# Weight splits ordered behind the attention steps, and output projections on spare wide PSUM tiles, in a streaming encoder on one core

## The chip, the cores and the metric

The program runs on one core of a Trainium2 chip. A core has a matmul engine, TensorE (PE, with its weight loads listed as PEld), and the engines VectorE (DVE), ScalarE (ACT), GpSimd (POOL) and SyncE (SP), each with an instruction stream of its own that it works through in order. They wait for each other by semaphores. PE writes its results to PSUM, which DVE and ACT read. The metric is the device time of one execution in microseconds. Before the change three executions took 1470.21, 1471.60 and 1471.62 us, a median of 1471.6.

## The reference

Two layers over 512 frames of one new stream and 16 frames of each of 8 running streams (640 columns in all, width 1024). The first layer is a convolution module, the second is chunked attention with 16 heads of 64; a SwiGLU feed-forward follows each. Everything is in float32. The attention layer, which is what the change touches, is this:

```
k, v = jnp.split(rms_norm(h, norm_kv) @ w_kv, 2, axis=-1)
q = (rms_norm(h, norm_attn[j]) @ w_q[j]).reshape(B, T, N_HEADS, HEAD_DIM)
s = einsum(q, k) * scale + bias        # own chunk of 64 frames and the 8 before
p = softmax(s)                         # chunks before the stream's start masked
o = einsum(p, v)
h = h + o @ w_o[j]
h = swiglu_ffn(h, norm_ffn[l], w_ffn_in[l], w_ffn_out[l])
```

The running streams attend to 512 cached rows of k and v each beside their own 16.

## The kernel before

Products in float32 accuracy are made of three matmuls on split operands: each weight w becomes `whi` (ACT, rounded) and `wlo` = w - `whi` (DVE), each activation `xh` and `xl`, and PE adds up whi·xh, wlo·xh and whi·xl. The residual stream `h` lies in SBUF as 8 tiles of 128 rows by 640 columns.

The attention layer goes through the 16 heads in 8 pairs, p = 0 to 7. The projections of pair 0 (k0, q0) and of the first group of values (v0) are made ahead. The others are made beside the attention: `SETS` lists 13 sets of weights, k (keys and queries of one pair), v (values of two pairs) and o (the output projection of two pairs, added to `h`). `stream()` is a generator that goes through them; each step of it issues one **piece** of PE's work on the present set and one or two pieces of the next set's split. The split is in `pieces()`: one DMA brings 1 MB of weights into `raw`, then 16 pieces of 128 columns (k) or 8 of 256 (v and o) go through `whi` on ACT (L1272 where the weight has no gain, L1276 where it has) and `wlo` on DVE (L1273, L1277). A k set has 12 pieces of PE's work, v 15, o 16 (one for each of 8 row tiles and two halves of 320 columns); a piece of o is six matmuls of 320 columns (L1259), a piece of k at most nine matmuls of 256 or 384.

`BO` is the order of one pair, and `FILL` says how many pieces go into each of the 8 pairs. In `BO`, f4 is "up to four pieces", f* "all that are left", and the rest are attention steps:

- A: `heads()`, the scores of both heads on two wide PSUM tiles and two narrow ones (L1396), from `KH`, `KL`, `QH`, `QL`, the split k and q of the pair (L1376, L1377). Then on DVE the bias and the row maximum (L1198) and `nb` (L1188), on ACT the exps (L1191), on DVE the scaling of `S` by `rs` (L1412).
- s0, s1: the scores of the running streams on a wide tile each (`Sn`, `Ss`, L1459, L1462).
- b00 to b12: transposes of `S` (L1425), copied to `PT` by ACT (L1429) or DVE (L1431).
- t0, t1 and n0, n1: transposes of `Sn` and `Ss` (L1475, L1481), copied to `PTs` by ACT (L1486) and to `PM` and `PN` by DVE (L1483).
- P, c, d: the products with the values (L1441, L1497), the last transpose (L1506), and the split of the result into `ohi` and `olo` (L187, L189).

PE's order is fixed by hand: each step is issued behind the last matmul of the step before (`pe()`, `step_end`). On the other engines a scheduler places the instructions by priority; the copies marked `high_priority` come first, the split pieces and the softmax come as the data allows. PSUM has two wide tiles (1024 columns, `w2t()`), two narrow tiles `mm` of 512 columns for the pieces (`mmt()`), and two `am` for transposes and the like. Between the step s1 and the next A no attention step uses the wide tiles. A piece of o takes an `mm` tile, and DVE adds it to `h` (L1344). At its first call, `stream()` loads the first set and splits all of it (`load(0)` and eight steps): the 16 pieces of k1. The last o set (o3) is made by `halves()` behind pair 7, on `mm` and `am` tiles; its `wlo` is one instruction of 2048 columns (L180).

With the sums of `FILL` (20, 42, 63, 87, 111, 137, 165, 177) and the sizes of the sets (k1 to 12, v1 to 27, k2 to 39, k3 to 51, o0 to 67, k4 to 79, v2 to 94, k5 to 106, o1 to 122, k6 to 134, v3 to 149, k7 to 161, o2 to 177), o0 lies with 12 pieces in pair 2 and 4 in pair 3, o1 with 5 in pair 4 and 11 in pair 5, o2 with 4 in pair 6 and 12 in pair 7.

Of the kernel before, what the change touches and what calls it, by code (L numbers as in the profile page):

```python
# [8 lines left out]
F32 = mybir.dt.float32  # L9
# [3 lines left out]
ALU = mybir.AluOpType  # L13
# [69 lines left out]
def tile_trunk(ctx, tc, xT, vecs, hist, w_pw1, w_pw2, w_in0, w_out0, w_os0, w_in1, w_out1, w_os1,  # L83
# [1101 lines left out]
    def softmax_rows(S, mx, sm, tiles):  # L1185
        k = len(tiles)
        nb = ap.tile([P, 4], F32, tag="nb", name=nm("nb"), bufs=3)
        nc.vector.tensor_scalar(out=nb[:, :k], in0=mx[:, :k], scalar1=-0.125, scalar2=None,  # L1188
                                op0=ALU.mult)
        for i, (o, n) in enumerate(tiles):  # L1190
            nc.scalar.activation(out=S[:, o:o + n], in_=S[:, o:o + n], func=AF.Exp, scale=0.125,  # L1191
                                 bias=nb[:, i:i + 1], accum_out=sm[:, i:i + 1])
# [9 lines left out]
    fill, step_end = None, [None]  # L1202

    def proj_kq(p):
        wh, wl = wsplit(w_kq[p], 16, P, gains=GKQ)
# [58 lines left out]
    def pieces(w, src, gains, n):  # L1264
        raw, hi, lo = (wp.tile([P, 2048], F32 if t == "raw" else F32R, tag=t, name=nm(t))
                       for t in ("raw", "whi", "wlo"))
        w += [hi, lo]
        nc.sync.dma_start(raw, src if len(src.shape) == 2 else src.rearrange("p m c -> p (m c)"))
        gains = gains or [(a, a + 256, None) for a in range(0, 2048, 256)]
        for i, (a, b, gain) in enumerate(gains):  # L1270
            if gain is None:
                nc.scalar.activation(out=hi[:, a:b], in_=raw[:, a:b], func=AF.Copy)  # L1272
                nc.vector.tensor_tensor(out=lo[:, a:b], in0=raw[:, a:b],  # L1273
                                        in1=hi[:, a:b].bitcast(F32), op=ALU.subtract)
            else:
                nc.scalar.activation(out=hi[:, a:b], in_=raw[:, a:b], func=AF.Copy, scale=gain)  # L1276
                nc.vector.scalar_tensor_tensor(out=lo[:, a:b], in0=raw[:, a:b], scalar=gain,  # L1277
                                               in1=hi[:, a:b].bitcast(F32), op0=ALU.mult,
                                               op1=ALU.subtract)
            if i % n == n - 1:  # L1280
                yield
        while True:
            yield

    def set_kq(p, w):
        wh, wl = w
        kt = op_.tile([P, NT], F32, tag="kt", name=nm("kt"), bufs=2)
        qt = op_.tile([P, NT], F32, tag="qt", name=nm("qt"), bufs=QB)
        kts[p], qts[p] = kt, qt
        for g, (g0, n) in enumerate(GR):  # L1290
            for t, dst in enumerate((kt, qt)):
                pt = mmt()
                for a, b in zip(PARTS, PARTS[1:]):
                    mm3_part(pt[:, :n], [(wh[:, (2 * k + t) * P:(2 * k + t + 1) * P],
                                          wl[:, (2 * k + t) * P:(2 * k + t + 1) * P])
                                         for k in range(KT)], xk(xs[g], range(KT)), a, b)
                    if b == KT:
                        with tc.high_priority(offset=HP):
                            nc.vector.tensor_tensor(out=dst[:, g0:g0 + n], in0=pt[:, :n],
                                                    in1=xs[g][2], op=ALU.mult)  # L1300
                            if g == 0 and t:
                                for hh in range(2):
                                    r = slice(hh * DH, hh * DH + DH)
                                    nc.gpsimd.tensor_copy(
                                        qbd[p % 2][r, :, hh, :],
                                        qt[r, 0:P].rearrange("p (b q) -> p b q", q=SB))
                        if g and t:
                            nc.sync.dma_start(k_out[p], kt)
                            split[p] = heads_split(p)
                    yield  # L1310

    def set_v(r, w):
        wh, wl = w
        VT = ap.tile([P, 5, 256], F32, tag="vt", name=nm("vt"), bufs=2)
        vts[r] = VT
        for tt in range(5):
            g = 0 if tt < 2 else 1
            c0 = tt * P - GR[g][0]
            pt = mmt()
            for a, b in zip(PARTS, PARTS[1:]):  # L1320
                mm3_part(pt[:, :256], [(xs[g][0][:, k, c0:c0 + P], xs[g][1][:, k, c0:c0 + P])
                                       for k in range(KT)],
                         [(wh[:, k * 256:(k + 1) * 256], wl[:, k * 256:(k + 1) * 256])
                          for k in range(KT)], a, b)
                if b == KT:
                    with tc.high_priority(offset=HP):
                        nc.scalar.activation(out=VT[:, tt, :], in_=pt[:, :256], func=AF.Copy,
                                             scale=xs[g][3][:, c0 // P:c0 // P + 1])
                    if tt == 4:
                        nc.sync.dma_start(v_out[:, :, r * 256:r * 256 + 256], VT)  # L1330
                yield

    def set_o(r, w):
        wh, wl = w
        for g0 in (0, NH):
            for m in range(KT):
                pt = mmt()
                mm3_part(pt[:, :NH], [(wh[:, (k * 8 + m) * P:(k * 8 + m + 1) * P],
                                       wl[:, (k * 8 + m) * P:(k * 8 + m + 1) * P])
                                      for k in range(2)],  # L1340
                         [(oT[2 * r + k][0][:, g0:g0 + NH], oT[2 * r + k][1][:, g0:g0 + NH])
                          for k in range(2)], 0, 2)
                with tc.high_priority(offset=HP):
                    nc.vector.tensor_tensor(out=h[:, m, g0:g0 + NH], in0=pt[:, :NH],  # L1344
                                            in1=h[:, m, g0:g0 + NH], op=ALU.add)
                yield
# [25 lines left out]
    def heads_split(p):  # L1372
        ts = [ap.tile([P, 512], F32R, tag=t, name=nm(t)) for t in ("KH", "KL", "QH", "QL")]
        with tc.high_priority(offset=HP):
            for src, hi, lo in ((kts[p], *ts[:2]), (qts[p], *ts[2:])):
                nc.scalar.activation(out=hi, in_=src[:, P:], func=AF.Copy)  # L1376
                nc.vector.tensor_tensor(out=lo, in0=src[:, P:], in1=hi.bitcast(F32),  # L1377
                                        op=ALU.subtract)
        return ts

    def heads(ts):
# [18 lines left out]
    def head_a(p, hh, pss):  # L1400
        S = sp.tile([P, 1280], F32, tag="S", name=nm("S"))
        mx = ap.tile([P, 4], F32, tag="mx", name=nm("mx"), bufs=3)
        sm = ap.tile([P, 4], F32, tag="sm", name=nm("sm"), bufs=3)
        for ii, i in enumerate(ORD):
            n = (i + 1) * P
            o = SOFF[i]
            addmax(S[:, o:o + n], pss[ii], BP[:, hh, 512 - n:512], mx[:, ii:ii + 1])
        rs = softmax_rows(S, mx, sm, [(SOFF[i], (i + 1) * P) for i in ORD])
        for ii, i in enumerate(ORD):
            n = (i + 1) * P  # L1410
            o = SOFF[i]
            nc.vector.tensor_scalar(out=S[:, o:o + n], in0=S[:, o:o + n],  # L1412
                                    scalar1=rs[:, ii:ii + 1], scalar2=None, op0=ALU.mult)
        return S

    def head_b(S, PT, j):
# [9 lines left out]
                        tr[:, o:o + P], S[:, SOFF[i] + k * P:SOFF[i] + (k + 1) * P], ident).ins  # L1426
                tot += P
        if j == 0:
            nc.scalar.activation(out=PT[:, base:base + tot], in_=tr[:, :tot], func=AF.Copy)  # L1429
        else:  # L1430
            nc.vector.tensor_copy(PT[:, base:base + tot], tr[:, :tot])  # L1431

    def pair_c(p, PTs):
        VT = vts[p // 2]
# [103 lines left out]
    for p in range(NP):  # L1538
# [8 lines left out]
        for op in BO.split():  # L1547
# [7 lines left out]
            i = int(op[1]) if len(op) > 1 else None  # L1555
            with pe(), tc.high_priority(offset=HP):
                if op[0] == "A":
                    pss = heads(split[p])
                    ha = {hh: head_a(p, hh, pss[hh]) for hh in range(2)}
                    pt = {hh: sp.tile([P, 1280], F32, tag="PT", name=nm("PT")) for hh in range(2)}  # L1560
# [11 lines left out]
                    ps[i]()  # L1572
                else:
                    pair_c(p, (pt[0], pt[1]))
            if op == "s1" and p + 1 < NP:
                bias_load(p + 1)

    next(fill, None)
    adds = []
# [228 lines left out]
```

## Time and profile before

| what | us |
|---|---|
| median of three runs | 1471.6 |
| profiled execution, own time | 1470.02 |
| its span | 1468.2 |
| PE busy in it | 1429.5 |
| attention stage, 691 to 1012 | 321.0, of which PE is busy 303.5 |

The other stages are the convolution layer and its feed-forward ahead of 633 us, the projections of pair 0 to 699, and the second feed-forward from about 1030 to the end. The granted clock over the span is 0.997 of the full one.

In the rows that follow, a row of a timeline gives start, duration, engine, line, operation, output<-inputs, shape and count, and in brackets the idle time of the engine just before it with what ended it. A row of instruction groups ends in busy time, mean duration in ns, and the idle time before the group with what released it. A row of waits gives engine, tile and line that waited, what for, and the total in us, the number of times and the longest. PE's durations overlap: the next matmul is issued before the last one ends.

### The profile page before, as it was taken

To read this page: it belongs to the slowest core of one execution; us is meant where nothing else is said; L and a number is where in the kernel's file an instruction comes from. 1 tells how busy PE (TensorE), PEld (TensorE's weight loads), DVE (VectorE), ACT (ScalarE), POOL (GpSimd) and SP (SyncE) were. 2 spreads that over 40 slices of the span, in tenths; PEclk is the share of its full clock that TensorE was granted. 3 is DMA by queue.
4 is the path that set the end of the run, shared out by engine and by line. 5 is a ranking of instruction groups with operands and counts; after the bars stand their busy time and mean duration, and the time that the engine had idled before them with its cause. 6 is when DMAs were issued, how large, how long until landed. Compare 5 with 4: busy or idle time off the path is not lost.

```text
span 1468.2 us, 28278 instructions
## 1 busy us (share of the span) xinstructions
PE 1429.5 (97%) x11086; PEld 1368.3 (93%) x11086; DVE 1119.1 (76%) x2509; ACT 748.2 (51%) x1633; POOL 281.5 (19%) x335
## 2 busy tenths in 40 slices
PE   9999999999999999999999999998999999999998
PEld 8998799999999999999888888887999999999998
DVE  6789767988788888666557657556899888788755
ACT  5666554554554554454544544433554455465453
POOL 5799130011110111012111111101001111111101
PEclk9999999999999999999999999999999999999999
DMA  7267434044545444415565464542124544544522
GB/s 242 85 172 185 120 87 144 19 134 144 133 107 149 130 110 121 137 58 200 172 201 163 157 208 156 187 143 62 68 77 133 137 118 125 144 120 108 157 63 72
DMA packets 66933, 192.58 MB, mean 131 GB/s; under 512 B 12144, under 2 KB 30320, under 8 KB 58480
## 3 DMA queue, kind: packets, MB, share of 16 engines
q1 hardware_dynamic: 52432, 160.58, 33.7%
q0 software_dynamic: 13504, 29.37, 10.1%
q8 instruction: 87, 1.43, 0.4%
q10 hardware_dynamic: 864, 0.83, 0.2%
q14 instruction: 46, 0.38, 0.1%
HBM read 179.14 MB, written 11.61 MB: 130 GB/s over the span
## 4 chain that ended last, share of the span: by engine, by line
PE 81%; DVE 10%; ACT 3%; DMA 3%; issue 1%; POOL 1%; DVEq 0%; ACTq 0%; POOLq 0%
PE mm L439 44%; PE mm L1259 9%; PE mm L199 6%; PE mm L200 6%; PE mm L201 6%; PE mm L885 2%; DMA raw<-in_w_os 2%; DVE wlo L372 1%; DMA raw<-in_w_in 1%; PE am L1441 1%; PE am L1497 1%; ACT whi L1276 1%; PE am L1425 1%; PE mm L146 1%; ACT S L1191 1%
## 5 line engine op out<-in xcount | busy, mean ns | idle before, releaser
L439 PE MATMUL mm<-XH,whi 128*128 128x320 f32 x896 | 276.0, 310 | 2.6 <-ACT t L451 2.6
L439 PE MATMUL mm<-XH,wlo 128*128 128x320 f32 x896 | 276.4, 309 | 0.0
L439 PE MATMUL mm<-XL,whi 128*128 128x320 f32 x896 | 274.7, 309 | 0.0
L371 ACT ACTIVATE whi<-raw 128x512 fp32r<-128x512 f32 (+2 forms) x280 | 168.4, 613 | 140.8 <-PE mm L439 107.4
L372 DVE TENSOR_TENSOR wlo<-raw,whi 128x512 fp32r<-128x512 f32 (+2 forms) x280 | 184.5, 667 | 19.0 <-ACT whi L371 17.9
L439 PE MATMUL mm<-hid,whi 128*128 128x320 f32 x732 | 172.0, 311 | 3.1 <-DVE hid L372 2.2
L439 PEld LDWEIGHTS mm<-XH,whi 128*128 128x128 f32 x896 | 167.8, 188 | 4.2 <-ACT t L451 4.2
L439 PEld LDWEIGHTS mm<-XH,wlo 128*128 128x128 f32 x896 | 168.3, 188 | 0.0
L439 PEld LDWEIGHTS mm<-XL,whi 128*128 128x128 f32 x896 | 167.8, 188 | 0.0
L439 PEld LDWEIGHTS mm<-hid,whi 128*128 128x128 f32 x732 | 125.0, 188 | 5.9 <-DVE hid L372 3.3
L199 PE MATMUL mm<-xh,whi 128*128 128x320 f32 (+2 forms) x416 | 129.2, 312 | 0.8 <-DVE h L702 0.4
L200 PE MATMUL mm<-xh,wlo 128*128 128x320 f32 (+2 forms) x416 | 128.1, 310 | 0.0
L201 PE MATMUL mm<-xl,whi 128*128 128x320 f32 (+2 forms) x416 | 126.0, 310 | 0.0
L439 PE MATMUL mm<-hid,wlo 128*128 128x320 f32 x366 | 113.1, 309 | 0.0
L439 PE MATMUL mm<-XH,shi 128*128 128x320 f32 x344 | 106.0, 309 | 0.7 <-DVE h L1528 0.7
L439 PE MATMUL mm<-XH,slo 128*128 128x320 f32 x344 | 106.1, 308 | 0.0
L439 PE MATMUL mm<-XL,shi 128*128 128x320 f32 x344 | 105.6, 308 | 0.0
L841 POOL TENSOR_TENSOR ca<-ca,cvt 128x512 f32<-128x512 f32 x60 | 91.9, 1531 | 16.3 <-ACT cvt L838 9.8
L417 POOL DMA_DIRECT2D s<-in_w_in x38 | 22.0, 580 | 377.1 <-DVE wlo L372 153.3
L371 ACT ACTIVATE shi<-raw 128x512 fp32r<-128x512 f32 (+1 forms) x114 | 66.7, 588 | 44.2 <-PE mm L439 39.3
L580 DVE TENSOR_TENSOR h<-h,mm 128x320 f32<-128x320 f32 x168 | 79.8, 480 | 4.3 <-PE mm L439 4.0
L451 ACT ACTIVATE t<-mm 128x320 f32<-128x320 f32 x114 | 49.5, 434 | 62.3 <-PE mm L439 61.9
(324 smaller groups left out, 3697.1 us busy)
## 6 DMA issues: line engine op xcount, KB each, us to landing
raw<-in_w_in SPq DMA_DIRECT2D x38, 1024.0 KB
s<-in_w_in POOLq DMA_DIRECT2D x76, 256.0 KB, 4.2
raw<-in_w_os SPq DMA_DIRECT2D x24, 768.0 KB
cache<-in_ck SPq DMA_DIRECT2D x32, 512.0 KB
cache<-in_cv SPq DMA_DIRECT2D x32, 512.0 KB
raw<-in_w_pw SPq DMA_DIRECT2D x11, 1024.0 KB
s<-in_w_os POOLq DMA_DIRECT2D x48, 192.0 KB, 3.6
raw<-in_w_kq SPq DMA_DIRECT2D x8, 1024.0 KB
```

Source lines behind the costliest of these rows:

```text
L199: nc.tensor.matmul(ps, wh, xh, start=(first and i == 0), stop=False)
L200: nc.tensor.matmul(ps, wl, xh, start=False, stop=False)
L201: end = nc.tensor.matmul(ps, wh, xl, start=False, stop=(stop and i == last))
L371: put_end[1] = nc.scalar.activation(out=hi, in_=src, func=AF.Copy).ins
L372: put_end[0] = nc.vector.tensor_tensor(out=lo, in0=src, in1=hi.bitcast(F32), op=sub).ins
L417: nc.gpsimd.dma_start(s1, src[:, 2 * n:3 * n])
L439: last = nc.tensor.matmul(pt, wt, v, start=(first and k == i == 0), stop=(k == n - 1 and i == 2), skip_group_check=True)
L451: keeps.append(nc.scalar.activation(out=t, in_=pt, func=AF.Copy).ins)
L580: nc.vector.tensor_tensor(out=hv, in0=hv, in1=pt, op=sub if row else add)
L841: nc.gpsimd.tensor_tensor(out=acc, in0=acc, in1=pr, op=ALU.add)
L885: conv_end[0] = nc.tensor.matmul(pt[32 * q:32 * q + 32, 0:n], w4[0:r, 4 * tg + q, :], mv, start=(tg == 0), stop=(tg == 7)).ins
L1259: step_end[0] = nc.tensor.matmul(ps, w, x, start=i == j == 0, stop=i == len(wts) - 1 and j == 2).ins
```

## The change

`note()` keeps, for each engine, the last instruction of the attention steps: the exps, the copies of `kt`, `qt` and `vt`, `KH`, `KL`, `QH`, `QL`, the scaling of `S` and the copies to `PT`. Each split piece is issued behind those kept ones (`behind`: an order on its own engine and against the others in the scheduler, with no semaphore of its own). Not kept are the copies to `PTs`, `PM` and `PN`, the bias and maximum, `ohi` and `olo`, and the adds to `h`. `set_o()` takes halves of a wide tile instead of an `mm` tile from the step s1 until the next A. `FILL` moves the sets between the pairs: its sums are now 20, 39, 67, 94, 122, 142, 165, 177, so that o0 lies wholly at the end of pair 2, o1 at the end of pair 4, and o2 as before.

```
-FILL = 20, 22, 21, 24, 24, 26, 28, 12
+FILL = 20, 19, 28, 27, 28, 20, 23, 12
...
-            nc.scalar.activation(out=S[:, o:o + n], in_=S[:, o:o + n], func=AF.Exp, scale=0.125,
-                                 bias=nb[:, i:i + 1], accum_out=sm[:, i:i + 1])
+            note(nc.scalar.activation(out=S[:, o:o + n], in_=S[:, o:o + n], func=AF.Exp,
+                                      scale=0.125, bias=nb[:, i:i + 1],
+                                      accum_out=sm[:, i:i + 1]))
...
+    fill, step_end, spare_w2 = None, [None], [None, []]
+    ahead = {}
+
+    def note(ins):
+        ahead[ins.ins.engine] = ins.ins
+        return ins
...
+            with behind(*ahead.values()):
+                if gain is None:
+                    nc.scalar.activation(out=hi[:, a:b], in_=raw[:, a:b], func=AF.Copy)
+                    nc.vector.tensor_tensor(out=lo[:, a:b], in0=raw[:, a:b],
+                                            in1=hi[:, a:b].bitcast(F32), op=ALU.subtract)
...
-                pt = mmt()
+                if spare_w2[0]:
+                    if not spare_w2[1]:
+                        t = w2t()
+                        spare_w2[1] += [t[:, 0:512], t[:, 512:1024]]
+                    pt = spare_w2[1].pop(0)
+                else:
+                    pt = mmt()
...
                 if op[0] == "A":
+                    spare_w2[:] = False, []
                     pss = heads(split[p])
...
+            if op == "s1":
+                spare_w2[0] = True
+                if p + 1 < NP:
+                    bias_load(p + 1)
```

The lines behind the edits move: L1259 becomes L1265, L1276 and L1277 become L1283 and L1284, L1272 becomes L1279, L1344 becomes L1357, L1376 and L1377 become L1389 and L1390, L1396 becomes L1409, L1425 becomes L1438, L1431 becomes L1444, L1486 becomes L1499.

ACT's order around pair 0's heads, before. `KH_7837` and `QH_7839` are the split k and q of pair 0, `whi_7952` is k1, `whi_8000` is v1, `S_7911` and `S_7930` are the scores of the two heads:

```order
L1376 ACTIVATE KH_7837<-kt_7576 128x512
L1276 ACTIVATE whi_7952<-raw_7951,vec 128x128 x12
L1376 ACTIVATE QH_7839<-qt_7577 128x512
L1276 ACTIVATE whi_7952<-raw_7951,vec 128x128 x4
L1238 ACTIVATE vt_7652<-mm_7758,rt_7465 128x256
L1238 ACTIVATE vt_7652<-mm_7784,rt_7465 128x256
L1276 ACTIVATE whi_8000<-raw_7999,vec 128x256 x2
L1238 ACTIVATE vt_7652<-mm_7810,rt_7465 128x256
L1191 ACT_TABLE_LOAD
L1191 ACTIVATE S_7911,sm_7913<-S_7911,nb_7918 128x512
```

The same engine and tiles in the changed kernel, from the second head's exps on (ahead of these rows stand `KH_7837`, `QH_7839`, two copies to `vt`, the table load and the five exps that come first):

```order
L1191 ACTIVATE S_7930,sm_7932<-S_7930,nb_7937 128x384
L1191 ACTIVATE S_7930,sm_7932<-S_7930,nb_7937 128x128
L1191 ACTIVATE S_7930,sm_7932<-S_7930,nb_7937 128x256
L1244 ACTIVATE vt_7652<-mm_7810,rt_7465 128x256
L1283 ACTIVATE whi_7952<-raw_7951,vec 128x128 x16
L1283 ACTIVATE whi_8000<-raw_7999,vec 128x256 x4
L1191 ACTIVATE Sn,sm_8047<-Sn,nb_8049 128x576
```

All 16 pieces of k1 have moved from ahead of the exps to behind them. DVE's `wlo` pieces have moved likewise, from ahead of the bias and maximum to behind the scaling of both heads. On PE the heads of pair 0 stand 16 matmuls earlier in the product of v0's fourth tile; the k1 matmuls stand where they stood, right behind v0's last.

ACT's order at the end of pair 2, before: `QH_9165` is the split q of the next pair, `whi_9184` the next set of weights, `PTs_9248` and `PTs_9267` the copies for the running streams:

```order
L1376 ACTIVATE KH_9163<-kt_8875 128x512
L1429 ACTIVATE PT_9003<-am_9134 128x512
L1276 ACTIVATE whi_9184<-raw_9183,vec 128x128 x12
L1376 ACTIVATE QH_9165<-qt_8876 128x512
L1276 ACTIVATE whi_9184<-raw_9183,vec 128x128 x4
L1429 ACTIVATE PT_9004<-am_9191 128x512
L1486 ACTIVATE PTs_9248<-am_9243 128x512
L1486 ACTIVATE PTs_9267<-am_9262 128x512
```

The same place in the changed kernel, with `whi_9200` as the next set and `PTs_9212` and `PTs_9230` as the copies:

```order
L1389 ACTIVATE KH_9179<-kt_8967 128x512
L1442 ACTIVATE PT_8966<-am_9150 128x512
L1389 ACTIVATE QH_9181<-qt_8968 128x512
L1283 ACTIVATE whi_9200<-raw_9199,vec 128x128 x13
L1499 ACTIVATE PTs_9212<-am_9207 128x512
L1283 ACTIVATE whi_9200<-raw_9199,vec 128x128 x3
L1499 ACTIVATE PTs_9230<-am_9225 128x512
```

`QH` and the second `PT` are now ahead of the pieces, and both `PTs` have pieces ahead of them, the first all thirteen.

PE's order in the pieces of o0, before. `mm_9505` and `mm_9513` are the PSUM tiles of two pieces that follow each other, `ohi` and `olo` the attention's split results:

```order
L1259 MATMUL mm_9505<-olo_7866,whi_8888 128x320
L1259 MATMUL mm_9505<-ohi_8407,whi_8888 128x320
L1259 MATMUL mm_9505<-ohi_8407,wlo_8889 128x320
L1259 MATMUL mm_9505<-olo_8408,whi_8888 128x320
L1259 MATMUL mm_9513<-ohi_7865,whi_8888 128x320 [waits DVE_49]
L1259 MATMUL mm_9513<-ohi_7865,wlo_8889 128x320
```

The pieces of o0 in the changed kernel, late in pair 2. `w_1016_9405` is a wide tile, and both halves of it carry its name:

```order
L1265 MATMUL w_1016_9405<-olo_7866,whi_8980 128x320
L1265 MATMUL w_1016_9405<-ohi_8407,whi_8980 128x320
L1265 MATMUL w_1016_9405<-ohi_8407,wlo_8981 128x320
L1265 MATMUL w_1016_9405<-olo_8408,whi_8980 128x320
L1265 MATMUL w_1016_9405<-ohi_7865,whi_8980 128x320 [waits DVE_49]
L1265 MATMUL w_1016_9405<-ohi_7865,wlo_8981 128x320
```

Before, the wait is for the add that reads the tile of the piece before the last one, since two `mm` tiles take turns. In the changed kernel the first matmul of the second half waits for the add that reads the first half of the same tile, because a wide tile is tracked as one. The next wide tile starts without a wait of its own.

More of the change, by code (lines that the diff above doesn't have):

```diff
@@ L1270, in pieces @@
         for i, (a, b, gain) in enumerate(gains):
[L1271 to L1279, printed above, removed]
+            with behind(*ahead.values()):
[4 more added lines that the diff above has]
+                else:
+                    nc.scalar.activation(out=hi[:, a:b], in_=raw[:, a:b], func=AF.Copy, scale=gain)
+                    nc.vector.scalar_tensor_tensor(out=lo[:, a:b], in0=raw[:, a:b], scalar=gain,
+                                                   in1=hi[:, a:b].bitcast(F32), op0=ALU.mult,
+                                                   op1=ALU.subtract)
             if i % n == n - 1:
@@ L1375, in heads_split @@
             for src, hi, lo in ((kts[p], *ts[:2]), (qts[p], *ts[2:])):
-                nc.scalar.activation(out=hi, in_=src[:, P:], func=AF.Copy)
-                nc.vector.tensor_tensor(out=lo, in0=src[:, P:], in1=hi.bitcast(F32),
-                                        op=ALU.subtract)
+                note(nc.scalar.activation(out=hi, in_=src[:, P:], func=AF.Copy))
+                note(nc.vector.tensor_tensor(out=lo, in0=src[:, P:], in1=hi.bitcast(F32),
+                                             op=ALU.subtract))
         return ts
@@ L1411, in head_a @@
             o = SOFF[i]
[L1412 to L1413 removed]
+            note(nc.vector.tensor_scalar(out=S[:, o:o + n], in0=S[:, o:o + n],
+                                         scalar1=rs[:, ii:ii + 1], scalar2=None, op0=ALU.mult))
         return S
```

16 lines of the change are left out of this document (7 added, 9 removed).

## The prediction

> **What bounds the kernel now.** I read the page's busy shares and its chain first, then the busy time of the attention stage by pair of heads, then what TensorE (PE) waited for there. The page:
>
> ```profile
> PE 1429.5 (97%) x11086; PEld 1368.3 (93%) x11086; DVE 1119.1 (76%) x2509; ACT 748.2 (51%) x1633; POOL 281.5 (19%) x335
> ...
> PE 81%; DVE 10%; ACT 3%; DMA 3%; issue 1%; POOL 1%; DVEq 0%; ACTq 0%; POOLq 0%
> ```
>
> PE is busy for 97% of the span. The diff touches only code between the first attention pair and the norm behind the last, so I took that stretch cut at the first head matmul of each pair 0 to 7 (columns: length, busy time of PE, PEld, DVE, ACT, POOL, granted clock, DMA share, GB/s):
>
> ```profile
> 693.00:735.00 42.00, 39.92 (x371) 35.00 (x370) 23.88 (x80) 21.85 (x59) 6.07 (x11) 0.96 0.53 172
> 735.00:773.00 38.00, 37.63 (x367) 33.34 (x365) 22.88 (x80) 19.26 (x60) 5.42 (x11) 1.00 0.63 211
> 773.00:811.00 38.00, 36.15 (x332) 31.05 (x334) 26.48 (x86) 16.17 (x49) 5.39 (x11) 1.00 0.52 164
> 811.00:853.00 42.00, 39.23 (x372) 34.66 (x370) 25.71 (x85) 19.61 (x58) 6.53 (x11) 1.00 0.54 186
> 853.00:892.00 39.00, 38.80 (x366) 34.13 (x364) 22.62 (x75) 18.38 (x56) 5.75 (x11) 1.00 0.52 172
> 892.00:937.00 45.00, 41.06 (x372) 36.10 (x370) 29.57 (x96) 18.93 (x55) 5.85 (x11) 1.00 0.47 156
> 937.00:981.00 44.00, 43.19 (x402) 38.64 (x402) 23.75 (x71) 18.51 (x49) 5.50 (x11) 1.00 0.54 173
> 981.00:1013.00 32.00, 26.46 (x266) 21.58 (x267) 19.39 (x64) 12.41 (x33) 3.04 (x4) 1.00 0.33 83
> ```
>
> Length less PE's busy time gives PE's idle time: 2.1, 0.4, 1.9, 2.8, 0.2, 3.9, 0.8 and 5.5 us, 17.6 us in all. That is everything the change can win by covering waits. What ended those waits (total, times, longest):
>
> ```profile
> PE mm L1259 <- DVE h L1344: 4.9, 4, 1.7
> PE am L1481 <- ACT PTs L1486: 2.8, 4, 1.9
> PE w L1396 <- DVE QL L1377: 2.2, 4, 1.2
> PE mm L1259 <- DVE nb L1188: 1.6, 2, 1.4
> PE w L1396 <- ACT QH L1376: 1.6, 2, 1.4
> ```
>
> They are what the change aims at: a projection piece that waits for the residual add h of an earlier piece, a transpose that waits for PTs, heads that wait for QH and QL, each with weight splits or softmax work ahead of it on ACT or DVE. PE issues in a fixed order, so each such wait delays all the rest. A wait costs a little more than its idle time:
>
> ```profile
> 814.48 0.31 PE L1259 MATMUL mm<-olo,whi 128*128 128x320 f32 x1
> 816.41 0.41 PE L1259 MATMUL mm<-ohi,whi 128*128 128x320 f32 x1 [1.62 <-DVE h L1344]
> ```
>
> These starts lie 1.93 us apart where the rows above them lie 0.147 apart (six matmuls, one piece, in 0.88 us): 1.78 us lost for 1.62 idle. So I add 0.16 us for each wait.
>
> **The change, part by part.** The same matmuls run; no work is added. Three things move.
>
> *First, the pieces of k1.* Before, they stood ahead of pair 0's softmax on ACT (twelve, QH, then four) and on DVE. The rows, of ACT, DVE and PE:
>
> ```profile
> 687.95 3.63 ACT L1276 ACTIVATE whi<-raw,vec 128x128 fp32r<-128x128 f32 x12 [2.79 <-PE mm L201]
> 691.49 0.62 ACT L1376 ACTIVATE QH<-qt 128x512 fp32r<-128x512 f32 x1
> ...
> 698.81 0.29 DVE L1188 TENSOR_SCALAR nb<-mx 128x4 f32<-128x4 f32 x2
> 699.56 0.45 ACT L1238 ACTIVATE vt<-mm,rt 128x256 f32<-128x256 f32 x1
> 700.03 1.28 ACT L1191 ACT_TABLE_LOAD   x1
> 701.33 0.72 ACT L1191 ACTIVATE S<-S,nb 128x512 f32<-128x512 f32 x1
> 705.62 0.18 ACT L1191 ACTIVATION_READ_ACCUMULATOR S<-S,nb 128x1 f32 x1
> 703.86 1.28 DVE L1412 TENSOR_SCALAR S<-S,rs 128x512 f32<-128x512 f32 x4
> 698.54 0.28 PE L201 MATMUL mm<-wlo,xh 128*128 128x256 f32 x1
> ```
>
> In the changed order all 16 stand behind both heads' exps on ACT and behind both heads' scalings on DVE, while PE's k1 matmuls still follow its last v0 matmul. PE is free there at 698.54 + 0.12 = 698.66. QH no longer waits behind twelve pieces, and the order shows the heads 16 matmuls earlier, 1.8 us; nb is ready near 697.3 then. Table load 1.28, the eight exps 705.80 - 701.33 = 4.47, a value copy 0.45: the first whi lands near 703.9. DVE scales the second head after its last exp (0.2 + 1.28) and makes the first wlo (0.35) by about 705.0; the second matmul needs it. PE waits about 5.2 us for whi and 0.9 more for wlo: **+6.1 us**. Ends: 4.9 (the wlo wait hidden) and 7.9 (heads where they stood). Everything on PE stands behind it. Afterwards pieces come every 0.30 us and PE takes one in 0.36, so it is not held again; the PTs wait of this pair, 1.9 us in 2.1 idle, goes (**-2.4**, two waits).
>
> A long gap also has a price in clock. PE's gap for PTs in pair 0 was followed by this (columns of the stretches as above):
>
> ```profile
> 723.13 0.33 PE L1481 MATMUL am<-ident,Sn 128*128 128x128 f32 x1 [1.93 <-ACT PTs L1486]
> ```
>
> ```profile
> 722.00:724.00 2.00, 0.71 (x4) 0.53 (x5) 1.52 (x7) 1.92 (x6) 0.00 (x0) 1.00 0.00 0
> 724.00:726.00 2.00, 2.00 (x11) 1.62 (x11) 0.27 (x1) 0.00 (x0) 0.00 (x0) 0.53 0.89 213
> 726.00:728.00 2.00, 2.00 (x8) 0.61 (x6) 0.00 (x0) 0.00 (x0) 0.00 (x0) 0.62 0.74 311
> ```
>
> (0.47 + 0.38) x 2 = 1.7 us lost. That spell goes with its gap, but the 6 us gap for k1 should bring one like it: **0**, ends -1.7 and +1.7 (two spells).
>
> *Second, o0 and o1, whole at the ends of pairs 2 and 4, on halves of the wide PSUM tiles.* In the order the second half of a wide tile waits for the add that reads the first half. Between them stands nothing on PE in the last tiles of the set. The add is this row, beside the matmul and a split piece:
>
> ```profile
> L1259 PE MATMUL mm<-ohi,whi 128*128 128x320 f32 x96 | 32.9, 342 | 6.7 <-DVE h L1344 4.9 <-DVE nb L1188 1.6
> L1344 DVE TENSOR_TENSOR h<-mm,h 128x320 f32<-128x320 f32 x48 | 22.9, 485 | 9.6 <-PE mm L1259 9.5
> L1277 DVE SCALAR_TENSOR_TENSOR wlo<-raw,vec,whi 128x128 fp32r<-128x128 f32 x107 | 31.1, 345 | 0.0
> ```
>
> From the last matmul of a half to the next piece: its 0.31, two handovers of some 0.05, the add's 0.485, less the ordinary 0.147: 0.75 us. Before, each piece had a tile of its own, and the wait was for the add of the piece before the last, so that a whole piece of 0.88 us covered it. Four tiles stand bare (3.0), a fifth has one transpose between its halves (0.6), one four (0.3), and the next heads wait for the last add (0.5): **4.4 us** for each set. Ends: 0, if the adds hold nothing, and 6.6 (all eight tiles bare and the heads).
>
> In the same pairs the next k set is split from the moment QH is through. ACT has thirteen pieces ahead of the first PTs, 13 x 0.303 = 3.9 us (3.63 for twelve, above). The four transposes that make its input and two pieces of PE's work take about 2.2 us of that; the next transpose waits **1.9 us**. DVE has up to fourteen wlo pieces and the adds ahead of the copy PM, and the other transpose waits **1.7 us** for it. Ends of the two: 0 and 5. Sum 8.0 us for pair 2 and again for pair 4, whose order reads the same: **+16.0**. The heads of pair 2 now come straight behind the last k2 piece. Rows for that (a copy of qt, QL, and the waits of pair 2 before):
>
> ```profile
> 790.58 0.56 DVE L1299 TENSOR_TENSOR qt<-mm,bc 128x384 f32<-128x384 f32 x1 [0.37 <-PE mm L1259]
> ```
>
> ```profile
> 980.88 0.68 DVE L1377 TENSOR_TENSOR QL<-qt,QH 128x512 fp32r<-128x512 f32 x1
> ```
>
> ```profile
> PE am L1425 <- DVE PT L1431: 0.8, 1, 0.8
> PE w L1396 <- DVE QL L1377: 0.6, 1, 0.6
> PE mm L1259 <- DVE h L1344: 0.4, 1, 0.4
> PE w L1396 <- ACT QH L1376: 0.2, 1, 0.2
> ```
>
> qt's copy, QH (0.62) and QL lie in the open: **+1.9**, in place of 1.3 (0.8 idle, a tail of 0.16 and a longer one of 0.33, since a head's matmul of 0.50 is followed by the next after 0.17).
>
> *Third, pairs 6 and 7.* The split:
>
> ```profile
> 978.68 2.28 DVE L180 TENSOR_TENSOR wlo<-raw,whi 128x2048 fp32r<-128x2048 f32 x1
> ```
>
> Before the heads of pair 7, DVE has adds of two half tiles between the split of the last output weights and small copies; the second half waits for the first's add behind them: 4.2 us by adding up that queue, in place of 1.2 idle + 0.3: **+2.7**, ends 0 and 5. Within pair 7 the wait of 1.7 stays (its four pieces are still on the narrow tiles), that of 1.4 becomes about 2.1 behind the scalings, and the two half pieces that filled the PTs wait stand earlier: **+1.5**, ends -1 and 3.
>
> What goes elsewhere, idle plus tails: pair 1 0.4; pair 2 1.6 and its heads 1.3; pair 3 3.3 (2.8 in three waits); pair 4 0.3; pair 5 and its heads 3.3; the heads of pair 6 2.1. With pair 0's 2.4 that is **-14.7**. What is late next there is nothing I can find: splits stand behind the steps, and a k or v piece follows wherever an add did.
>
> The sum: 6.1 + 16.0 + 1.9 + 2.7 + 1.5 - 14.7 = **+13.5 us**. The profiled execution took 1470.0, its span 1468.2; it lies 1.6 below the median of 1471.6 and at the low edge of the runs. 1470.0 + 13.5 = 1483.5, 1485.1 from the median; I take **1484**.
>
> **A rule to weigh.** The half clock above came 1.9 us into a gap, while the gaps of 1.62 at 816 and 1.7 at 987 brought none. [...]
>
> **Rivals.** *More half clock*: the waits of 1.9 us in pairs 2 and 4 and that ahead of pair 7 each bring a spell of 1.7, and k1's gap a second one. For: 1.93 did; against: 1.7 did not. Up to 6.8 more, 1488 to 1493; likeliest 1488.
>
> *A wash*: half of the tile and PTs terms is covered because ACT and DVE reach pairs 2 and 4 earlier than I time them (DVE is idle for 11.5 and 16.4 us of them in the rows above). Then 16.0 becomes 8.0 and the last pairs nothing: +1 to +5, 1471 to 1475.
>
> *Faster*: the adds hold nothing. If both halves of a wide tile can be filled without the add between them, the tile waits fall in pairs 2 and 4 (8.8), with them the queue that PM stands in (3.4), and pair 7's two terms (4.2): 13.5 - 16.4 = -2.9, 1467; with the narrowest k1 wait 1465.9. It decides at the 0.75 us: whether a second half starts before the first's add ends. Against: the order names that wait seven times in a row.
>
> *It does not do what it says*: pieces "one by one" still stand thirteen in a row on ACT; that is in the forecast.
>
> **Chances.** 0.2%, about what a measurement of this kernel can tell from no change, is 2.9 us. The forecast (1476 to 1488) 0.54, more half clock 0.22, the wash 0.13 (0.08 of it within 2.9 us), faster 0.11 (0.02 of it within). So faster 0.09, same 0.10, slower 0.81. The range takes in the rivals but for the faster one and the far end of the spells: 1471 to 1493.
>
> **What would show it.** In the changed profile: a PE wait of 5 to 7 us for whi or wlo near 699, with a half clock behind it (first part right); no wait for PTs in pair 0; waits of 0.5 to 0.6 us for h, a dozen of them, near 800 and 885 (second part); PTs and PM waits just before; no h waits in pairs 3 and 5. I am wrong if k1's matmuls start before 702, if the second halves follow the first at 0.15 us, or if h is awaited for longer than an add takes.

## The result and the profile after

The changed kernel takes 1489.6 us (median of four, 1487.7 to 1491.5) against 1471.6: the ratio is 1.0123, 95% interval 1.0106 to 1.0141, slower by 18.0 us. The forecast was +13.5 us and 1484, with a range of 1471 to 1493. The profiled execution took 1491.5 us, its span 1489.7. The page of the changed kernel, engines and chain:

```profile
PE 1438.9 (97%) x11086; PEld 1373.5 (92%) x11086; DVE 1120.5 (75%) x2509; ACT 746.9 (50%) x1633; POOL 281.6 (19%) x335
...
PE 83%; DVE 9%; DMA 4%; ACT 2%; issue 1%; POOL 1%; DVEq 0%; ACTq 0%; POOLq 0%
```

PE does the same 11086 matmuls and is "busy" 9.4 us longer. As the work is the same, that is a slower clock (0.991 granted over the span in place of 0.997), or matmuls that overlap less. Again by pair, cut at the heads (length, busy PE, PEld, DVE, ACT, POOL, granted clock, DMA share, GB/s):

```profile
693.00:741.00 48.00, 42.07 (x385) 37.40 (x385) 26.88 (x87) 25.32 (x71) 5.66 (x11) 0.93 0.39 130
741.00:776.00 35.00, 34.65 (x343) 30.52 (x341) 21.44 (x76) 17.22 (x54) 5.81 (x11) 1.00 0.68 226
776.00:827.00 51.00, 44.60 (x372) 37.37 (x373) 31.20 (x100) 18.99 (x58) 6.30 (x11) 0.97 0.49 161
827.00:870.00 43.00, 42.85 (x406) 38.63 (x404) 24.09 (x80) 20.57 (x59) 6.22 (x11) 1.00 0.48 163
870.00:920.00 50.00, 44.56 (x376) 37.66 (x375) 29.88 (x94) 18.38 (x56) 6.29 (x11) 0.97 0.47 154
920.00:956.00 36.00, 35.85 (x349) 31.66 (x347) 22.76 (x74) 18.69 (x53) 6.22 (x11) 1.00 0.41 130
956.00:997.00 41.00, 38.13 (x363) 33.50 (x361) 24.24 (x74) 17.18 (x48) 5.97 (x11) 1.00 0.67 226
997.00:1033.00 36.00, 30.17 (x272) 23.94 (x273) 18.72 (x62) 13.01 (x34) 3.04 (x4) 0.95 0.24 63
```

By this cut the attention stage grew from 320 to 340 us. Of that, 1.9 us come from the cut itself: the first head matmul now stands 16 matmuls earlier in v0, 26.7 us behind the last matmul of the first feed-forward (`mm<-hid`) in place of 28.6. From that last matmul to the first one of the norm behind the stage (`w<-onec,sqs`), which is the same work in both kernels, the time grew by 17.6 us, from 358.6 to 376.2. The stage's idle time by pair is now 5.9, 0.4, 6.4, 0.2, 5.4, 0.2, 2.9 and 5.8 us, 27.1 in place of 17.6. Pairs 3 and 5, which had idled 2.8 and 3.9, hardly do; pairs 0, 2 and 4 have taken their place. PE's waits there:

```profile
PE w L1265 <- DVE h L1357: 10.0, 14, 2.4
PE mm L1265 <- ACT whi L1283: 5.4, 1, 5.4
PE am L1494 <- ACT PTs L1499: 4.1, 4, 1.5
PE am L1494 <- DVE PM L1496: 2.1, 2, 1.0
...
PE mm L1265 <- DVE h L1357: 1.4, 1, 1.4
PE w L1409 <- ACT QH L1389: 1.1, 1, 1.1
...
PE mm L1265 <- DVE wlo L1284: 0.6, 1, 0.6
```

The first is new: pieces on the wide tiles (`w`) that wait for the add, 14 times. The second and the last are k1's. The view runs from 690 to 1050 us. One wait of the first kind in PE's timeline, late in pair 2, from the last matmul of a first half to the first of the second:

```profile
817.97 0.31 PE L1265 MATMUL w<-olo,whi 128*128 128x320 f32 x1
818.86 0.42 PE L1265 MATMUL w<-ohi,whi 128*128 128x320 f32 x1 [0.58 <-DVE h L1357]
```

The starts are 0.89 us apart where 0.147 is ordinary: 0.74 us lost, against 0.75 forecast. The clock, behind k1's wait and in pair 2:

```profile
706.00:708.00 2.00, 1.02 (x3) 0.73 (x4) 2.00 (x8) 2.00 (x8) 0.00 (x0) 0.50 0.29 102
708.00:710.00 2.00, 2.00 (x11) 2.00 (x11) 2.00 (x9) 2.00 (x8) 0.00 (x0) 0.50 0.69 234
...
806.00:808.00 2.00, 2.00 (x8) 0.65 (x8) 0.49 (x1) 0.00 (x0) 0.00 (x0) 0.56 0.82 184
808.00:810.00 2.00, 2.00 (x14) 0.92 (x10) 0.00 (x0) 0.00 (x0) 0.00 (x0) 0.58 0.81 340
```

There are such spells behind the waits of pairs 0, 2 and 4 and ahead of pair 7 (from 703.9 us for 6.8 us, and from 806.2, 898.4 and 997.4 for 3.4 us each), where before there was one in pair 0 (from 724.1 for 3.4 us).

### The profile page after: what moved, and what is told of

Its sections match the earlier page's. It is cut to its first block, busy times and chain, and to the rows that moved or that the text cites. A ratio compares the mean times of both kernels' runs of the same rounds, so it can differ in the third digit from the quotient of the medians.

```text
span 1489.7 us, 28266 instructions
## 1 busy us (share of the span) xinstructions
PE 1438.9 (97%) x11086; PEld 1373.5 (92%) x11086; DVE 1120.5 (75%) x2509; ACT 746.9 (50%) x1633; POOL 281.6 (19%) x335
## 4 chain that ended last, share of the span: by engine, by line
PE 83%; DVE 9%; DMA 4%; ACT 2%; issue 1%; POOL 1%; DVEq 0%; ACTq 0%; POOLq 0%
PE mm L439 43%; PE mm L1265 10%; PE mm L199 5%; PE mm L200 5%; PE mm L201 5%; PE w L1265 2%; PE mm L885 2%; DMA raw<-in_w_os 2%; DMA raw<-in_w_in 2%; PE am L1454 1%; DVE wlo L372 1%; PE am L1510 1%; PE am L1438 1%; PE w L1409 1%; PE mm L146 1%
## 5 line engine op out<-in xcount | busy, mean ns | idle before, releaser
L580 DVE TENSOR_TENSOR h<-h,mm 128x320 f32<-128x320 f32 x168 | 80.1, 482 | 3.6 <-PE mm L439 3.4
L422 DVE TENSOR_TENSOR raw<-raw 128x512 f32<-128x512 f32 (+1 forms) x62 | 39.6, 639 | 55.9 <-DMA raw<-in_w_in 43.5
```

The lines of the kernel that those rows point to most:

```text
L422: nc.vector.tensor_tensor(out=a21, in0=a11, in1=a21, op=add)
L580: nc.vector.tensor_tensor(out=hv, in0=hv, in1=pt, op=sub if row else add)
```

## The experiments

Times are medians; beside each stands its ratio to the kernel before, measured on the same chip in the same session. The medians of before in those sessions lay between 1468.7 and 1469.8 us, some 2 to 3 us under the 1471.6 of the first session, so a difference of medians between sessions holds that shift as well. The edits act only between the last matmul of the first feed-forward and the first of the norm. In the profiled executions the part ahead of this stretch, which no edit touches, ended between 663.3 and 666.8 us. So the length of the stretch, one profiled execution each, tells best what an edit did:

| kernel | stretch, us |
|---|---|
| before | 358.6 |
| changed | 376.2 |
| 1, k1 first | 370.1 |
| 2, narrow tiles | 361.4 |
| 3, no order | 377.2 |
| 4, gaps filled with 12 and 8 | 379.9 |
| 5, gaps filled with 6 and 4 | 372.8 |
| 6, one piece a tile | 365.5 |
| 7, k1 first and narrow tiles | 353.6 |
| 8, PTs, PM and PN kept | 344.0 |
| 9, order alone | 349.4 |
| 10, run 8 with the old FILL | 347.0 |
| 11, three pieces moved | 339.8 |
| 12, norm's gap filled | 339.8 |

**1. k1's pieces ahead of the softmax.**

```
+    def pieces(w, src, gains, n, tied=True):
...
+            with behind(*(ahead.values() if tied else ())):
...
+            return w, pieces(w, src(r), gains, n, i > 0)
```

> The changed kernel, but the first set's split pieces (k1) are not ordered behind the attention steps, so they stand ahead of pair 0's softmax again. My theory: the 6.1 us wait near 699 and the half clock behind it (1.7) go, and no PTs wait comes back in pair 0, since k2's pieces stay behind: 1489.6 - 7.8 = 1481.8 us (1480 to 1484). Rival (the wait only moves: pair 0 waits elsewhere, as it did before for PTs, 2.4 and a half clock): 1486 to 1490.

1480.6 us, ratio 1.0073 (1.0058 to 1.0088): 9.0 less than the changed kernel by the medians, 6.1 in the stretch. The wait for `whi` and its half clock are gone, and pair 0 has no wait for PTs. From the start of the stretch to the heads of pair 1 the kernel is 8.3 us shorter. Of these, 1.4 come back in pair 2, where PE now waits for a `PT`, and 0.9 in pair 7, where it waits for the maximum and the half clock lasts longer (6.8 us in place of 3.4). So the wait was removed for the most part and moved for the rest:

```profile
PE w L1265 <- DVE h L1357: 9.4, 14, 2.4
...
PE am L1494 <- DVE PM L1496: 2.1, 2, 1.0
...
PE am L1438 <- ACT PT L1442: 1.2, 1, 1.2
PE w L1265 <- DVE mx L1199: 1.2, 1, 1.2
```

**2. The output projections on narrow tiles again.** `spare_w2[0]` is never set.

> The changed kernel, but the output projections take the narrow PSUM tiles again, one piece a tile; orders and FILL as changed. My theory: the waits of second halves go (4.4 us in each of pairs 2 and 4, about 4 around pair 7, with a half clock of 1.7 ahead of pair 7); the waits for PTs and PM in pairs 2 and 4 stay: 1489.6 - 14.5 = 1475 us (1472 to 1479). Rival (DVE is late with the adds anyway, because split pieces stand before them, so narrow tiles wait too): 1483 to 1488.

1470.4 us, ratio 1.0007 (0.9995 to 1.0019): no longer slower than before. By the medians it is 19.2 us less than the changed kernel; in the stretch it is 14.8, against 14.5 expected. The waits of PE between 773 and 1000 us:

```profile
PE am L1494 <- ACT PTs L1499: 3.7, 2, 1.9
PE mm L1265 <- DVE h L1357: 2.6, 2, 1.6
PE am L1494 <- DVE PM L1496: 2.0, 2, 1.0
```

The fourteen waits on wide tiles are gone; those for PTs and PM remain, as they should.

**3. No order: wide tiles and the new FILL alone.** `note()` keeps nothing.

> The changed kernel without the order behind the attention steps (note keeps nothing): wide tiles and the new FILL alone. My theory: k1's wait goes with its half clock (-7.8), pair 0's PTs wait and half clock of before come back (+4.1), the tile waits stay, and PTs in pairs 2 and 4 stand behind sixteen pieces instead of thirteen (+0.9 each): 1489.6 - 1.9 = 1488 us (1483 to 1491). Rival (the order edges are what costs): below 1480.

1488.2 us, ratio 1.0125 (1.0108 to 1.0142), as expected. The order edges by themselves are not what makes the change slow. Its waits:

```profile
PE am L1493 <- ACT PTs L1498: 10.8, 12, 1.9
PE w L1264 <- DVE h L1356: 10.3, 16, 2.4
PE w L1408 <- ACT QH L1388: 3.2, 1, 3.2
```

Without the order, PTs is awaited twelve times in place of four over the same 690 to 1050 us, and QH for 3.2 us. What the order saves here is about what k1's wait costs: with k1 exempt the order shortens the stretch by 7.1 us (runs 3 and 1), and k1's pieces behind the steps add 6.1 (run 1 and the changed kernel).

**4. Idle matmuls in the gaps of pairs 2 and 4.** Their results are not read.

```
+            if op[0] == "n" and p in (2, 4):
+                with pe(), tc.high_priority(offset=HP):
+                    step_end[0] = warm((12, 8)[i])
```

> The changed kernel with 12 and 8 matmuls of 128 columns that nobody reads ahead of the two transposes that wait for PTs and PM in pairs 2 and 4 (about 1.4 and 0.9 us of work in gaps of 1.5 and 1.0). If half clock is set off by PE's idle time there, the spells near 807 and 899 go: 1489.6 - 3.4 = 1486.2 us, with the profile's clock at 1.0 there. If the idle time is not what sets it off, the spells stay: 1489 to 1491.

1490.8 us, ratio 1.0144 (1.0122 to 1.0166), where 1486.2 was expected. There were no spells in pairs 2 and 4 (clock 1.00 from 713 to 996 us), but PE's timeline shows what ate the gain:

```profile
802.86 2.84 PE L146 MATMUL mm<-ident 128*128 128x128 f32 x24
805.54 0.27 PE L1494 MATMUL am<-ident,Sn 128*128 128x128 f32 x1
805.65 1.95 PE L146 MATMUL mm<-ident 128*128 128x128 f32 x16
807.44 0.27 PE L1494 MATMUL am<-ident,Ss 128*128 128x128 f32 x1
```

Each of these matmuls has two records and takes 0.225 us; I had reckoned half of that. The second transpose was issued at 807.44, and P began 30.9 us behind the pair's first head in place of 29.4 (at 808.52 and 806.14): 1.5 us later, about what the missing spell of half clock gave back. Pairs 2 and 4 took 50.9 and 50.3 us in place of 51.0 and 50.4. That the stretch is 3.7 longer lies in pairs 0, 6 and 7, where half clock lasted longer than in the changed kernel: some 6.1 us while PE worked in pair 0 (from 706.0 on), 6.8 from 996.2 and 3.4 from 1026.9, in place of 3.7 in pair 0 and 3.4 from 997.4.

**5. The same with 6 and 4.**

> As the run that filled the gaps, with 6 and 4 idle matmuls, since each took 0.225 us there and twenty of them overran the gaps by 1.4 us. If PE's idle time sets half clock off: no spell near 807 and 899, pairs 2 and 4 each 1.5 to 1.7 us shorter than in the changed kernel (51.0 and 50.4 before), 1489.6 - 3.2 = 1486.4 us. If not: spells there, 1489 to 1490.

1484.8 us, ratio 1.0115 (1.0096 to 1.0134): 4.8 less than the changed kernel by the medians, but the intervals of the two ratios overlap, so the time alone shows no gain. The stretch is 3.4 us shorter, as expected. Pairs 2 and 4, from head to head, took 49.3 and 48.7 us in place of 51.0 and 50.4. The clock in P's matmuls of pair 2:

```profile
803.00:805.00 2.00, 2.00 (x13) 0.86 (x13) 0.49 (x1) 0.00 (x0) 0.00 (x0) 1.00 0.71 172
805.00:807.00 2.00, 2.00 (x27) 1.51 (x26) 0.67 (x2) 0.60 (x1) 0.00 (x0) 1.00 0.85 356
```

The waits as such are as long as before, only filled; what went is the half clock, 1.7 us in each pair, and that is the whole 3.4. The single executions lie between 1484.1 and 1489.8.

**6. One piece for each wide tile.** Only the first half of a spare tile is used, `spare_w2[1] += [t[:, 0:512]]`.

> The changed kernel, but each spare wide tile takes one piece (its first half only), so no piece shares a tile with the one before. If the waits come from two pieces sharing a tile: like the run on narrow tiles, 1470 us (1467 to 1475), and no wait for h in pairs 2 and 4 but small ones. If the wide tiles themselves are the matter (where they lie, or the heads that want them next): 1482 to 1489.

1474.6 us, ratio 1.0030 (1.0014 to 1.0046). The fourteen waits are gone with the sharing, so it is the shared tile that costs, not the wide PSUM as such. It lies 4.2 above the narrow tiles, in the median and in the stretch, and the trace has two waits that they don't: for a copy `olo` ahead of pair 7's heads, and for the maximum.

```profile
PE w L1409 <- DVE olo L189: 2.2, 1, 2.2
...
PE w L1265 <- DVE mx L1199: 0.8, 1, 0.8
```

**7. k1 first and narrow tiles together.**

> k1's pieces ahead of pair 0's softmax and o pieces on narrow tiles; the order and the new FILL kept. If the two costs add up: 1470.4 - 9.0 = 1461.4 us (1460 to 1465), faster than before. If the one hides the other: 1467 to 1470.

1463.3 us, ratio 0.9959 (0.9945 to 0.9973). The two costs add up (22.6 us in the stretch, 6.1 and 14.8 singly), and with both gone the remainder of the change is a gain.

**8. PTs, PM and PN kept as well.** Run 7 with two more calls of `note()`, so that later split pieces stand behind these copies:

```
+        note(nc.scalar.activation(out=PT, in_=tr, func=AF.Copy))
         return rest
...
+            note(nc.vector.tensor_copy(pn[v0:, :], tn[v0:, 0:P]))
```

> As the run with k1 first and narrow tiles, and the copies PTs, PM and PN are also kept, so that later split pieces stand behind them (two and two pieces ahead of the PTs in pairs 2 and 4 instead of thirteen and three). If PTs and PM waited for pieces: 2.9 us a pair and a half clock of 1.7 go in pairs 2 and 4, 1461.4 - 9.2 = 1452 us (1451 to 1457). If they waited for something else, or the next set comes late: 1459 to 1463.

1454.7 us, ratio 0.9905 (0.9891 to 0.9920); the stretch is 9.6 us shorter than in run 7, against 9.2 expected. The waits left are others:

```profile
PE mm L1265 <- DVE h L1357: 1.6, 1, 1.6
PE w L1611 <- DVE sqs L1604: 1.6, 1, 1.6
PE w L1409 <- DVE QL L1390: 1.5, 2, 1.3
PE mm L1265 <- DVE nb L1188: 1.5, 1, 1.5
PE w L1409 <- ACT QH L1389: 1.1, 1, 1.1
PE am L1438 <- ACT PT L1442: 1.1, 1, 1.1
PE am L1494 <- ACT PTs L1499: 0.8, 2, 0.6
```

PM is no longer awaited, and PTs only in pair 7.

**9. The order alone, with the old FILL and k1 exempt.**

> The kernel before with the order behind the attention steps alone (k1 exempt): old FILL, narrow tiles, PTs not kept. It tells whether the order by itself is a gain. My theory: pair 0's PTs wait and half clock go (-4.1), QH and QL are no longer behind splits ahead of pairs 5 and 6 (-2), PTs in pairs 2, 4, 5 and 6 stand behind up to fourteen pieces (+1 to +3): 1469 - 4 = 1465 us (1461 to 1468). Rival (the order costs wherever it acts): 1470 or more.

1459.2 us, ratio 0.9929 (0.9914 to 0.9944), better than expected. I had counted waits for PTs behind up to fourteen pieces; the trace has none outside pair 7. In pair 2 of this kernel the k3 set ends three pieces earlier, so its weights are free earlier. On ACT the next set's split begins 3.5 us ahead of the transposes that PTs is copied from (784.46 and 787.96); in run 7 it begins 0.2 behind them (790.01 and 789.78). So the pieces ahead of PTs are done in time. What remains are the adds, as before:

```profile
PE mm L1265 <- DVE h L1357: 6.6, 8, 1.7
```

**10. Run 8 with the old FILL.**

> As the fastest version so far (k1 first, narrow tiles, PTs, PM and PN kept), with the old FILL. If the new places of the o sets are worth something with narrow tiles: slower than 1454.7, 1456 to 1460 us. If they are worth nothing: 1453 to 1456.

1459.2 us, ratio 0.9924 (0.9904 to 0.9944): 4.5 us behind run 8 by the medians, 3.0 in the stretch, with intervals that overlap a little. So on narrow tiles the new places of the o sets look like a gain once PTs is kept; without that they were a loss (run 7 against run 9, 1463.3 and 1459.2, and 4.2 in the stretch). With the old FILL, keeping PTs changes nothing in the median (runs 9 and 10). The stretch is 2.3 shorter, of which 1.4 are a wait for `nb` in pair 7 that the edit doesn't aim at.

**11. Three k3 pieces moved to the end of pair 1.** Run 8 with FILL = 20, 22, 25, 27, 28, 20, 23, 12.

> As the fastest version so far, with three k3 pieces moved from pair 2 to the end of pair 1 (FILL 20, 22, 25, 27, 28, 20, 23, 12), so that they lie between the last k2 piece and the heads that wait for QH and QL. If that wait is the copies standing in the open: 1.9 us go, 1454.7 - 1.9 = 1452.8 us (1451.5 to 1454.5). If the pieces only move another wait into pair 2: 1454 to 1456.

1450.9 us, ratio 0.9872 (0.9857 to 0.9887), 3.8 less than run 8 (4.2 in the stretch) and a little under the expected span. Three of its waits are gone: that for QH and QL ahead of pair 2 and, which I had not counted, that of 1.1 us for PT within it, and the one of 1.5 us for `nb` in pair 7. Pairs 1 and 2 together are 2.9 us shorter, which is the work of the moved pieces. The other 1.4 lie in pair 7, which the edit doesn't aim at: there DVE has four adds ahead of the scalings, in run 8 two. Left are:

```profile
PE w L1611 <- DVE sqs L1604: 1.6, 1, 1.6
PE mm L1265 <- DVE h L1357: 1.6, 1, 1.6
PE w L1409 <- DVE QL L1390: 1.3, 1, 1.3
```

**12. Idle matmuls ahead of the norm.** Run 11 with six matmuls that nobody reads in the 1.58 us wait for `sqs`, on the same tile:

```
         st, nt = w2t(), len(tiles(NH))
+        for _ in range(6):
+            nc.tensor.matmul(st[:, 0:P], ident, ident, start=True, stop=True)
```

> As the fastest version so far (three pieces moved), with six idle matmuls of 128 columns on PE ahead of the sum of squares that waits 1.58 us before the second feed-forward (6 x 0.225 = 1.35 us). That wait is in every run, with a half clock of 3.4 us behind it. If PE's idle time sets it off: no half clock near 1006, 1450.9 - 1.7 = 1449.2 us (1448.5 to 1450). If not, or if the idle matmuls delay the sum: 1450.5 to 1452.

1449.7 us, ratio 0.9862 (0.9845 to 0.9878). The interval overlaps that of run 11, so the time alone doesn't separate them. In the traces the stretch is the same, and from the norm to the end this run takes 437.0 us in place of 438.7, 1.7 less, as expected. The clock, first in run 11, then in this run:

```profile
1005.00:1007.00 2.00, 2.00 (x11) 2.00 (x11) 1.65 (x4) 0.00 (x0) 1.09 (x1) 0.59 0.37 63
1007.00:1009.00 2.00, 2.00 (x11) 2.00 (x9) 1.45 (x3) 0.00 (x0) 0.63 (x1) 0.56 0.84 299
```

```profile
1005.00:1007.00 2.00, 2.00 (x14) 1.82 (x14) 1.75 (x3) 0.00 (x0) 1.43 (x1) 1.00 0.48 127
1007.00:1009.00 2.00, 1.74 (x14) 1.66 (x14) 1.69 (x4) 0.44 (x1) 0.29 (x1) 1.00 0.92 309
```

The four executions of this run have granted clocks of 0.998 to 1.000, those of run 11 0.997 to 0.998. The expectation's "in every run" is not quite so: in runs 2 and 5 the same wait, 1.6 us in both, brought no half clock (1.00 from 995 us to 1060).

## Why the prediction was right, and where it was off

- **k1's wait** was forecast at 6.1 us; PE waited 5.4 for `whi` and 0.6 for `wlo`. Run 1 shows that it is the order that causes it. The 2.4 us for PTs in pair 0 went as forecast.
- **The shared wide tiles** were forecast at 0.75 us a bare tile; the rows show 0.74. Runs 2 and 6 show the cause by two ways. Without the shared tiles the change is no slower than before (run 2), though k1's wait is still in it. For a whole set 4.4 us were forecast; the rows of pair 2 have five waits, 2.8 us idle and 3.6 with their tails, and 0.2 at most at the next heads.
- **PTs and PM** in pairs 2 and 4 were forecast at 1.9 and 1.7 us; the rows have 1.5 and 1.0 idle, 1.6 and 1.2 with their tails. Run 8 removes them by taking the pieces out from before the copies. So the mechanism stands and the size was a fifth to two fifths too large. The step behind it, that pieces ahead of PTs always delay it, was too simple: in run 9 fourteen of them cost nothing; they began earlier.
- **Heads of pair 2**: 1.9 us forecast; in the rows 1.1 for QH and 0.2 for QL, some 1.8 with the tails that the prediction works with. Run 11 removes them by three pieces between.
- **Pair 7**: 2.7 us more were forecast ahead of its heads and 1.5 within it. Idle time grew by 1.7 ahead of the heads (waits of 0.47 and 2.39 for `h` in place of 1.20 for QL) and by 0.2 within (1.39, 1.10, 0.37 and 1.01 in place of 1.69, 1.37 and 0.60).
- **Removed**: pairs 1, 3 and 5 and the heads of pair 6 lost their waits, as forecast; those pairs idle for 0.2 to 0.4 us.
- **The half clock** is the term that was mis-sized. The sum had it at 0: one spell gone, one come. The profiled execution has four spells in the attention stage. Of half clock while PE worked they hold 3.7 us in pair 0, from 706.4 on and without the wait for `wlo`, and about 3.4 each in pair 2, in pair 4 and ahead of pair 7, 13.9 us in all, of which half is lost at a clock of 0.50: 7.0 us against 1.7 before, **+5.3**. I had priced this as a rival, 1488 likeliest, with a chance of 0.22; it is what came. The weighing counted gaps of 1.62 and 1.7 us that brought no spell; it left out one of 1.57 ahead of the norm, at 1022 us of the kernel before, with half clock from 1024.5 on. For pairs 2 and 4 the spell hangs on the gaps: of the ten pairs of gaps of 1.5 to 1.9 and 1.0 us that the traces of the changed kernel and of runs 1, 2, 6 and 7 have there, nine were followed by half clock, and of the four that runs 4 and 5 filled none.

Adding up: idle time rose by 9.5 us, half clock by 5.3, together 14.8 of the 17.6 by which the stretch grew in the profiled execution. The tails of the waits (36 in place of 29 by my count of gaps between matmuls, at 0.16 each) make some 1.1 more; the last 2 us or so I could not assign to single places. So the sum came near in part by luck: its waits were some 3 us too large, idle time and tails taken together, and its half clock 5.3 too small.

Behind the stage, the remainder of the span grew from 455.2 to 456.7 us. The trace has one wait there, of 2.58 us at 1138, that no other trace has at that place, with 3.4 us of half clock behind it. The add that PE waited for (`h`, L580) stands on DVE behind an instruction that waited 2.41 us for weights to land (`raw`, `in_w_os`). So far as the traces show, this belongs to the one execution, the slowest of the four, and not to the change.

The prediction weighed the length of the gap; by length alone the traces do not settle which gap brings half clock. A gap of 1.58 us ahead of the norm (1.57 in the kernel before) was followed by it in eleven of the thirteen traces that have it, those of the kernel before and of run 11 among them; in the trace of run 12, which fills it, there is none; in pairs 2 and 4 it was two gaps of 1.5 and 1.0 us with one transpose between; one of 1.62 us at 816 us of the kernel before brought none. In the changed kernel the spells behind these gaps last 3.4 us each.

The rival that ended on the faster side did not come. Its deciding point, whether a second half starts before the first's add ends, was read rightly from the order. What it leaves out is that the rest of the change is a gain: without the shared tiles and without k1 the same kernel is at 1463.3, and with two more kept copies and three pieces moved at 1450.9, 1.28% faster than before.

## What to carry to other kernels

Halves of one PSUM tile are no second buffer where dependencies are tracked by tile: two pieces that share one wait for each other's evacuation, here 0.74 us each time; with tiles of their own the fourteen waits went. An order edge that keeps background work behind the steps of a chain has to be checked for the first round, whose work is needed at once, and for every copy of the chain that it leaves out. A stall of PE may cost twice its length by the clock behind it (here 1.58 us and 1.7 more, run 11 against run 12); where the stall can't go, idle matmuls that fit into it may keep the clock up, as they did here (1.00 in runs 5 and 12).

## What the runs showed of the hardware that I had not expected

Half clock came after gaps of 1.58 us (norm), 1.93 (pair 0 before) and 1.46 + 1.03 (pairs 2 and 4), but not after one of 1.62 at 816 us of the kernel before. The same gaps don't always bring it: in run 7 those of pair 2 (1.87 and 1.03 us) did, and the equal ones of pair 4 did not.

The clock records of this case's traces show a step. In the changed kernel the spells of half clock between 640 and 1060 us start at 703.85, 806.25, 898.41, 997.40 and 1045.18 us, which is 30, 27, 29 and 14 times 3.413 us apart. The two spells of the kernel before (724.1 and 1024.5) lie 88 such steps apart, those of run 1 (796.5, 888.6, 987.6 and 1035.4) 27, 29 and 14, and in all nine traces with more than one spell there the starts lie whole steps apart, as near as windows of 1 us tell. Each spell there lasts 3.41 us or two or three times that (6.83 from 703.85 on in the changed kernel, 10.2 from 700.2 on in run 2). So in these traces a spell starts at one of these steps and not a set time behind its gap: it came 0.9 us behind the end of the norm's gap in the kernel before and 2.2 us behind it in the changed one. What decides whether a gap brings half clock stays open: both gaps of 1.87 us in run 7 lie whole between two steps (by the same windows they end 0.36 us ahead of a step in pair 2 and 0.03 in pair 4), and one brought it, the other not.

The length varies in these steps. The spell ahead of pair 7 lasted 3.4 us in the changed kernel and twice that in run 1 (987.6 to 994.4 us), where the same wait of 2.4 us came before it. That may be one source of the spread between single executions of one kernel: those of the changed kernel, with granted clocks of 0.991 to 0.994, span 3.8 us, those of run 11, with clocks of 0.997 to 0.998 and one spell there in the profiled one, 0.9 us. It is not the only one, since the part ahead of the stage ends up to 3.5 us apart.
